# State-space layer on one Trainium2 core: its units sooner, one GELU over its output in place, GpSimd putting it in order

## The chip, the cores and the metric

The kernel runs on one core of a Trainium2 chip, in a single launch. The metric is device time in microseconds (us), lower is better. Three runs of the kernel before took 2256.18, 2250.8 and 2256.09 us (median 2256.09).

## The reference

One layer of a hybrid trunk over 2048 tokens of width 1024, in float32. A normalised input is projected; 512 of the projected columns go through a diagonal complex state-space scan (32 channel groups of 16), 1536 are queries, keys and values of chunked attention with 8 heads. Both outputs are normalised, joined and projected, and a SwiGLU feed-forward follows.

```python
states = associative_scan(combine, (lam_bar, b_bar @ u))     # per group: 64 complex states
y = Re(c_mat @ states) + d_skip * u
y = gelu(y)
y = y * sigmoid(y @ w_glu + b_glu)                           # GLU
x = x + concat(rmsnorm(y), rmsnorm(attention)) @ w_out
x = x + (silu(h2 @ w_gate) * (h2 @ w_up)) @ w_down
```

## The kernel before

Every product runs as three matmuls on values that are split into a high and a low part (fp32r), so TensorE (PE) carries most of the work. A split is a cast by ScalarE (ACT), which writes the high part, and a subtraction by VectorE (DVE), which writes the low part (`split`, L153). PE's instructions run in the order in which the program is written; those of the other engines are put in order when the kernel is built, and each engine then works through its own list strictly in turn.

The middle of the program is `att_phase`: 128 attention steps (4 blocks of 512 tokens, 4 pairs of heads, 2 heads, 4 query tiles), about 4 us each. For a step, PE computes scores (tile `sc`), DVE adds a bias and takes the minimum (`s`, `mn`, L874), ACT takes the exponential (L877); two steps later PE transposes the result (`pt`, L79, a single buffer), ACT casts it (`pth`, L892) and DVE forms the rest (`ptl`, L893). Every fourth step there are 16 matmuls with the values (`pj`), whose halves ACT and DVE add (`yt` L916, `ya` L917). Since `pt` has one buffer, PE's transposes of a step wait for the `ptl` of the step before.

Between these, in each step, `Unit.advance` runs pieces of other work on PE ("units"): the projections of later blocks (`pf`), and the state-space layer in 8 units of 4 groups each. A state-space unit has a front (`ssm_front`): SP loads its input `U` and a matrix `Bst`, PE runs 4 matmuls, ACT copies the result into `X` (8 copies, L584), GpSimd (POOL) scans `X` in place (L598 to L610) and sends the states to `XG` (L632, DMA); and a back (`ssm_back`): matmuls of `U` and `XG`, ACT copies the result over `U` (L652), and a DMA writes it to `y` in HBM (L654). `X`, `XG`, `U`, `Bst` have one buffer each; the input of units 2, 4 and 6 lies in `rsn`, a tile of another phase. The tables `SX` and `SY` (L661, L662) give the steps at which the fronts and backs start. SP issues all loads and most stores from one queue, in list order.

From step `OPEN` = 119 on, the first pieces of the next phase (`mix_phase`) run as units inside the last attention steps: the pool `aw` (projection weights and hidden tiles such as `hi0x`, `lo0x`) is released, 512 KB by 512 KB `y` is fetched into `yr` (4 DMAs, L1046), gate weights `sg` are loaded and split (`wgh`, `wgl`), and from step `GSTART` = 122 on a block of 512 tokens is taken with one GELU (L1058) that also turns the layout from (j, chunk) to (chunk, j):

```python
nc.scalar.activation(yt[:, s].rearrange("p f (c j) -> p f c j", j=L), yv[:, s].rearrange("p f j c -> p f c j"), AF.Gelu_apprx_tanh)
```

It reads one element in 128. The result `ys` is split into `gh` and `gl`, and `glu` (16 pieces, 3 matmuls each on `pf`) follows; `ya` loads bring the attention output, whose squares (`sq`, `sg`, L1031 to L1035) feed a norm. The GELU and the exponential need different tables on ACT, so each change brings an ACT_TABLE_LOAD. The next block's GELU comes four steps later. Behind the last step PE goes on with tile `big`.

Of the kernel before, what the change touches and what calls it, by code (L numbers as in the profile page):

```python
# [10 lines left out]
F32R = mybir.dt.float32r  # L11
# [5 lines left out]
P = 128  # L17
# [5 lines left out]
L = 8  # L23
NC = SEQ // L
# [8 lines left out]
LAG = 2  # L33
NSMALL = 100
WB = 3
OPEN, GSTART = 119, 122
R1 = 13
SGB = 2
RA1, RA2 = 2, 12
QS = 4, 5, 6, 7, 0, 1, 2, 3  # L40
HTA = -12, -9
HTS = -8, -6
# [51 lines left out]
def f32(ap):  # L94
    return ap.bitcast(F32)
# [462 lines left out]
        yield  # L558


def ssm_front(k, p, psum, S, b, eng):

    nc = k.nc

    def load(out, in_):
        ins = nc.sync.dma_start(out, in_)
        if b == 0:
            k.tc.keep_in_program_order(ins)

    U = S["rsn"][:, : GB * NC].rearrange("p (g c) -> p g c", g=GB) if b and b % 2 == 0 else k.t(p, "U", [P, GB, NC])[:]  # L570
    k.U[b] = U
    load(U.rearrange("p g t -> p (g t)"), S["u"].rearrange("j (c g) n t -> (j c) (g n t)", c=CH)[:, GB * NC * b : GB * NC * (b + 1)])
    bst = k.t(p, "Bst", [P, GB, P])
    load(bst[:].rearrange("p g m -> p (g m)"), S["bst"][b // 2][:, (b % 2) * GB * P : (b % 2 + 1) * GB * P])
    yield

    X = k.t(p, "X", [P, 2, GP, NC])
    for q in range(GP):
        ps = k.t(psum, "pj", [P, 2, NC], bufs=2)
        for g2 in range(2):  # L580
            k.ta.matmul(ps[:, g2, :], bst[:, 2 * q + g2, :], U[:, 2 * q + g2, :], start=True, stop=True)
        for g2 in range(2):
            for c in range(2):
                nc.scalar.copy(X[g2 * NS : (g2 + 1) * NS, c, q, :], ps[c * NS : (c + 1) * NS, g2, :])  # L584
        yield

    a8 = S["a8"]
    qs = slice(GP * b, GP * b + GP)
    Xk = X[:].rearrange("p r q (k s) -> p r q k s", s=8)
    Xe = Xk[:, :, :, :, 7].rearrange("p r q (a b) -> p r q a b", b=8)  # L590

    def step(dst, src, e, n):

        ar = a8[:, 0, qs, (0, 7, 15)[e]].unsqueeze(1).to_broadcast([P, 2, GP]).unsqueeze(3).to_broadcast([P, 2, GP, n])
        aw = S["sw"][:, e, :, qs].unsqueeze(3).to_broadcast([P, 2, GP, n])
        t = k.t(p, "st1", [P, 2, GP, NC // 8])
        t2 = k.t(p, "st2", [P, 2, GP, NC // 8])
        eng.tensor_tensor(t[:, :, :, :n], src, ar, op=ALU.mult)  # L598
        eng.tensor_tensor(t2[:, :, :, :n], src[:, ::-1], aw, op=ALU.mult)
        eng.tensor_tensor(dst, dst, t[:, :, :, :n], op=ALU.add)  # L600
        eng.tensor_tensor(dst, dst, t2[:, :, :, :n], op=ALU.add)

    def carry(dst, end, i0, n):

        for c in range(2):
            for e in range(2):
                t = k.t(p, "fx", [P, GP, NC // 8, 7])[:, :, :n]
                pw = a8[:, c if e == 0 else 1 - c, qs, i0 : i0 + 7].unsqueeze(2).to_broadcast([P, GP, n, 7])
                eng.tensor_tensor(t, end[:, e].unsqueeze(3).to_broadcast([P, GP, n, 7]), pw, op=ALU.mult)
                eng.tensor_tensor(dst[:, c], dst[:, c], t, op=ALU.subtract if e == 1 and c == 0 else ALU.add)  # L610
# [12 lines left out]
    yield from carry(Xk[:, :, :, 1:, :7], Xk[:, :, :, : NC // 8 - 1, 7], 0, NC // 8 - 1)  # L623

    if b == 0:
        k.XG = k.t(p, "XG", [P, GB, NC])
        nc.gpsimd.memset(k.XG[:, :, 0:1], 0.0)
    XG = k.XG
    XGv = XG[:].rearrange("p (q g) c -> p q g c", g=2)
    for g2 in range(2):  # L630
        for c in range(2):
            eng.dma_start(XGv[c * NS : (c + 1) * NS, :, g2, 1:], X[g2 * NS : (g2 + 1) * NS, c, :, : NC - 1])  # L632
    yield


def ssm_back(k, p, psum, S, b):

    nc = k.nc
    gs = slice(GB * b, GB * b + GB)
    tm = k.t(p, "Tm", [P, GB, P])  # L640
    nc.sync.dma_start(tm[:], S["tm"][:, gs])
    vm = k.t(p, "Vm", [P, GB, P])
    nc.sync.dma_start(vm[:], S["v"].rearrange("q g c n m -> (c n) (q g) m")[:, gs, CH:])
    yield
# [13 lines left out]
SSM_F = 1 + GP + 7 + 7 + 3 + 4 + 1  # L658
SSM_B = 1 + GP + 1
ST = 2, 10  # L660
SX = 4, 24, 35, 48, 61, 74, 87, 100  # L661
SY = 20, 36, 49, 62, 75, 88, 101, 114  # L662


class Unit:
# [21 lines left out]
def att_phase(k, ident, S, aw, x0, roots):  # L687

    tc, nc, io, pfs = k.tc, k.nc, k.io, k.pfs
    with ExitStack() as cx:  # L690
# [271 lines left out]
        k.U = {}  # L962
        units.append(Unit(shifted_taps(k, S), L, *ST))
        for b in range(NG // GB):
            units.append(Unit(ssm_front(k, sp, psum, S, b, k.ssm_eng), SSM_F, SX[b], SX[b] + 9, SX[b] - 2 if b == 0 else 2 if b == 1 else 5, light=SL))
            units.append(Unit(ssm_back(k, sp, psum, S, b), SSM_B, SY[b], SY[b] + 2, 6, light=SL))
        N = len(steps)
        for s in range(N + LAG + 2):
            if s == OPEN:
                aw.release()  # L970
                mix = mix_phase(k, S, lambda: k.t(pfs, "pf", [P, 512]))
                units += [Unit(islice(mix, MIX_N), MIX_N, GSTART, N + LAG, GSTART - OPEN)]
            if s == GSTART:
                sp.release()
# [12 lines left out]
        yield mix  # L987


PY, PZ = 8, 1  # L990
MIX_N = 17 + PY + PZ


def mix_phase(k, S, bank):
# [3 lines left out]
    with ExitStack() as cx:  # L998
# [49 lines left out]
        def load(sb, one=False):  # L1048
# [4 lines left out]
            if sb and sb % 2 == 0:  # L1053
                fetch(sb)
            yv = b.yr = yrs[0][:, :, :, (sb % 2) * 64 : (sb % 2 + 1) * 64]
            fs = [slice(0, 4)] if one else [slice(f, f + 1) for f in range(4)]
            for s in fs:
                nc.scalar.activation(yt[:, s].rearrange("p f (c j) -> p f c j", j=L), yv[:, s].rearrange("p f j c -> p f c j"), AF.Gelu_apprx_tanh)  # L1058
# [91 lines left out]
            yield  # L1150

        def next_block(sb):
            b = load(sb)
            load_a(b, sb)
            for _ in glu(b, big):
                pass
            return b
# [7 lines left out]
                for i in range(8):  # L1165
                    yield t[:, i * SB : (i + 1) * SB]

        fetch(0)
        load_wg()
        yield  # L1170
        mw = rx.enter_context(tc.tile_pool(name="mw", reuse_waits="tile", bufs=2, side="right"))
        wr = rx.enter_context(tc.tile_pool(name="wr", reuse_waits="tile", bufs=2, side="right"))
        b = load(0, True)
        load_a(b, 0)
        raws = [load_wo(n, wr, "xt") for n in range(2)]
        for _ in range(PY):
            yield
        for n, _ in enumerate(glu(b, bank, True)):
            if n == RA1:
                rstd1(b, 0, bank())  # L1180
            if n == RA2:
# [1 line left out]
                spread(k, te, pb, b.o[0], 0)  # L1183
                rstd2(b, 0, pb[:])
            yield
        nxt = load(1, True)
        for _ in range(PZ):
            yield

        def bk():  # L1190
            nonlocal psum
# [554 lines left out]
```

## Time and profile before

| | |
|---|---|
| profiled execution | 2247.43 us |
| its span | 2245.7 us (1.7 us lie around it) |
| median of 3 runs | 2256.09 us |
| PE, DVE, ACT, POOL busy | 2155.6, 1543.3, 1004.6, 352.4 us |
| mean granted TensorE clock | 0.988 |

The prediction quotes the rows. In a row of the timeline stand the start in us from the span's start, the duration, engine, line, operation, tiles (out<-in) and shape, and in brackets how long the engine had been idle before it and whom it waited for. In a row of windows stand the stretch, its length, the busy time of PE, PE's weight loads, DVE, ACT and POOL with their instruction counts, the granted TensorE clock (1.00 is full), the share of the DMA engines and GB/s.

### The profile page before, as it was taken

What the parts mean: (1) busy time and instruction counts of PE and PEld (TensorE: products, weight loads), DVE (VectorE), ACT (ScalarE), POOL (GpSimd) and SP (SyncE); (2) the same over time, 40 slices, a digit from 0 to 9 for tenths busy, and PEclk for the clock granted to TensorE, in tenths of its full rate; (3) what the DMA queues carried; (4) which work ended last, traced back from release to release, by engine and by line L of the source; (5) the groups of instructions that cost most, each with busy time, mean ns of one, the idle gap of its engine ahead of it and who ended that gap; (6) DMA issues with size and microseconds to landing.
All of it is one profiled execution on the core that took longest, in us unless ns stands there. A gap on an engine that the chain in (4) does not pass through costs nothing.

```text
span 2245.7 us, 30154 instructions
## 1 busy us (share of the span) xinstructions
PE 2155.6 (96%) x10632; PEld 1817.4 (81%) x10632; DVE 1543.3 (69%) x2706; ACT 1004.6 (45%) x1667; POOL 352.4 (16%) x827
## 2 busy tenths in 40 slices
PE   8998899999997999999999999999999999999997
PEld 6777788899986788788888887888888788888886
DVE  7756666555557766777766678767666477689776
ACT  5455555556557642443333335333333343353322
POOL 2246576656500000000000000000000100000000
PEclk9999999999998999999999999999999999999999
DMA  8878876666652435845655557646333395465652
GB/s 281 251 244 275 280 220 204 202 192 199 190 166 99 155 113 181 288 136 155 198 168 194 191 182 268 210 144 213 117 100 112 122 383 192 160 228 177 220 175 76
DMA packets 194744, 430.16 MB, mean 192 GB/s; under 512 B 19872, under 2 KB 38352, under 8 KB 187488
## 3 DMA queue, kind: packets, MB, share of 16 engines
q1 hardware_dynamic: 186944, 403.32, 54.4%
q0 software_dynamic: 7648, 24.92, 3.6%
q8 instruction: 83, 1.36, 0.2%
q14 instruction: 69, 0.57, 0.1%
HBM read 288.95 MB, written 131.10 MB: 187 GB/s over the span
## 4 chain that ended last, share of the span: by engine, by line
PE 81%; DVE 7%; DMA 4%; ACT 3%; issue 2%; SPq 0%; DVEq 0%; ACTq 0%
PE X L76 20%; PE ps L76 19%; PE Y L76 10%; PE pf L76 10%; PE big L76 7%; PE W L76 5%; PE pj L76 4%; PE pt L79 2%; PE sc L76 2%; DMA lo<-hc 1%; DMA xt<-in_xt 1%; DVE ptl L893 1%; DMA x<-xt 0%; DVE s L874 0%; DVE lo L153 0%
## 5 line engine op out<-in xcount | busy, mean ns | idle before, releaser
L76 PE MATMUL X<-hi,c 128*128 128x512 f32 x1408 | 449.8, 390 | 6.7 <-DVE c L153 3.9
L76 PE MATMUL ps<-hd,hd 128*128 128x512 f32 (+1 forms) x1968 | 428.1, 379 | 3.1 <-DVE hd L153 2.0
L76 PEld LDWEIGHTS ps<-hd,hd 128*128 128x128 f32 x1968 | 356.4, 188 | 73.3 <-DVE hd L153 2.7
L76 PEld LDWEIGHTS X<-hi,c 128*128 128x128 f32 x1408 | 264.5, 188 | 63.2 <-DVE c L153 4.7
L76 PE MATMUL X<-lo,c 128*128 128x512 f32 x704 | 274.4, 390 | 0.0
L153 ACT CAST hd<-hd 128x1536 fp32r<-128x1536 f32 (+1 forms) x106 | 147.5, 1394 | 229.9 <-DMA hd<-hq 175.5
L76 PE MATMUL Y<-hi,c 128*128 128x512 f32 x704 | 224.8, 390 | 3.1 <-DVE u L1421 2.5
L153 DVE TENSOR_TENSOR hd<-hd 128x1536 fp32r<-128x1536 f32 (+1 forms) x106 | 174.0, 1643 | 38.0 <-ACT hd L153 37.7
L153 DVE TENSOR_TENSOR c<-S,c 128x512 fp32r<-128x512 f32 x176 | 120.8, 687 | 100.1 <-ACT c L153 99.8
L1525 POOL DMA_DIRECT2D hd<-hq x7 | 5.3, 755 | 1161.5 <-PE X L76 1148.8
L1417 ACT COPY u<-X 128x512 f32<-128x512 f32 x132 | 77.3, 586 | 197.7 <-PE X L76 197.7
L153 ACT CAST c<-S 128x512 fp32r<-128x512 f32 x176 | 109.4, 621 | 120.5 <-PE Y L76 61.6
L76 PE MATMUL big<-m,woh 128*128 128x512 f32 x512 | 160.1, 394 | 0.0
L76 PEld LDWEIGHTS Y<-hi,c 128*128 128x128 f32 x704 | 132.4, 188 | 31.9 <-DVE u L1421 3.3
L1559 DVE TENSOR_TENSOR acc<-acc,ps 128x512 f32<-128x512 f32 x196 | 129.6, 680 | 37.3 <-PE ps L76 37.1
L76 PEld LDWEIGHTS X<-lo,c 128*128 128x128 f32 x704 | 132.4, 188 | 27.4
L76 PE MATMUL pf<-hi,w 128*128 128x512 f32 x416 | 149.3, 411 | 0.0
L153 ACT CAST c<-raw 128x512 fp32r<-128x512 f32 x132 | 82.2, 623 | 147.7 <-PE Y L76 70.6
L76 PE MATMUL Y<-lo,c 128*128 128x512 f32 x352 | 137.2, 390 | 0.0
L893 DVE TENSOR_TENSOR ptl<-pt,pth 128x640 fp32r<-128x640 f32 (+3 forms) x152 | 98.2, 646 | 55.2 <-ACT pth L892 53.8
L877 ACT ACTIVATE s<-s,mn 128x640 f32<-128x640 f32 (+4 forms) x128 | 98.0, 765 | 61.1 <-DVE mn L874 57.7
L892 ACT CAST pth<-pt 128x640 fp32r<-128x640 f32 (+3 forms) x152 | 83.6, 550 | 84.2 <-PE pt L79 79.5
(448 smaller groups left out, 4267.9 us busy)
## 6 DMA issues: line engine op xcount, KB each, us to landing
w<-wss SPq DMA_DIRECT2D x36, 1024.0 KB, 6.1
hq<-g SPq DMA_DIRECT2D x140, 256.0 KB, 2.1
hd<-hq SPq DMA_DIRECT2D x35, 768.0 KB, 4.4
hd<-wc SPq DMA_DIRECT2D x35, 768.0 KB, 5.9
raw<-in_w_gate SPq DMA_DIRECT2D x44, 512.0 KB, 3.7
raw<-in_w_up SPq DMA_DIRECT2D x44, 512.0 KB, 4.1
wc<-px SPq DMA_DIRECT2D x66, 256.0 KB, 3.4
wss<-w SPq DMA_DIRECT2D x12, 1024.0 KB, 6.0
```

Of the source, the lines that this page charges most:

```text
L76: return self.tc.keep_in_program_order(self.tc.nc.tensor.matmul(*a, **b))
L79: return self.tc.keep_in_program_order(self.tc.nc.tensor.transpose(*a, **b))
L153: return nc.scalar.copy(hi, raw), nc.vector.tensor_tensor(lo, raw, f32(hi), op=ALU.subtract)
L877: nc.scalar.activation(s[:, :nk], s[:, :nk], AF.Exp, bias=mn[:], scale=-1.0, accum_out=sums[sb, pr][:, hh, qp : qp + 1])
L892: nc.scalar.copy(pth[:, a:b, qp, :], pt[:, a:b, :])
L893: nc.vector.tensor_tensor(ptl[:, a:b, qp, :], pt[:, a:b, :], f32(pth[:, a:b, qp, :]), op=ALU.subtract)
L1417: nc.scalar.copy(u[:], ps[:])
L1525: (nc.gpsimd if aside else nc.sync).dma_start(f32(lo), src.rearrange("g p c -> p g c"))
L1559: V.tensor_tensor(a, a, ps[:], op=ALU.add)
```

## The change

1. The state-space units start sooner. Unit 1's input goes into two dead tiles of `aw` (`hi0x`, `lo0x`, 2 DMAs) and is read a second time into `U` at its back, so its front can run before unit 0's back; all later fronts and backs move ten steps up, with loads four steps ahead.
2. At step 107 the pool of the state-space units is released and `y` for the first 1024 tokens is fetched into a new tile `y0` (4 DMAs, L987); at step 111 one GELU runs over all of it in place, 128x4096 (L989), pinned in program order.
3. `take` (POOL copies of 128x512, L1079) replaces the two GELUs of the first two blocks; `glu` starts at step 121 with three pieces before the `y0` pool is given back and the `ya` loads come. The second block's split comes after the GLU.

```diff
-OPEN, GSTART = 119, 122
+FETCH, OPEN, GSTART = 107, 119, 121
-RA1, RA2 = 2, 12
+RA0, RA1, RA2 = 3, 10, 14
...
-    U = S["rsn"][:, : GB * NC].rearrange("p (g c) -> p g c", g=GB) if b and b % 2 == 0 else k.t(p, "U", [P, GB, NC])[:]
+    if b == 1:
+        us = [lent(q).rearrange("p (g c) -> p g c", g=2) for q in range(GP)]
+        for q in range(GP):
+            load(us[q], ssm_input(S, b, slice(q, q + 1)))
+    else:
...
 def ssm_back(k, p, psum, S, b):
+    if b == 1:
+        k.U[b] = k.t(p, "U", [P, GB, NC])[:]
+        nc.sync.dma_start(k.U[b], ssm_input(S, b))
...
-SX = 4, 24, 35, 48, 61, 74, 87, 100
-SY = 20, 36, 49, 62, 75, 88, 101, 114
+SX = 4, 19, 31, 42, 54, 66, 78, 91
+SY = 20, 32, 43, 55, 67, 79, 92, 104
...
+            if s == FETCH:
+                sp.release()
+                k.my0 = tc.alloc_tile_pool(name="my0", reuse_waits="tile", bufs=1)
+                k.y0 = k.t(k.my0, "y0", [P, 4, L, 128])
+                for f in range(4):
+                    nc.sync.dma_start(k.y0[:, f], S["y"][:, f * P : (f + 1) * P, :128].rearrange("j p t -> p j t"))
+            if s == FETCH + 4:
+                tc.keep_in_program_order(nc.scalar.activation(k.y0[:], k.y0[:], AF.Gelu_apprx_tanh))
...
-MIX_N = 17 + PY + PZ
+MIX_N = 19
...
+                if sb < 2:
+                    nc.gpsimd.tensor_copy(yo, yv[:, f].rearrange("p j c -> p c j"))
+                else:
+                    nc.scalar.activation(yo, b.yr[:, f].rearrange("p j c -> p c j"), AF.Gelu_apprx_tanh)
...
-        fetch(0)
         load_wg()
+        yrs[0] = k.t(my, "yr", [P, 4, L, 128])
+        b = load(take(0))
+        nxt = take(1)
         yield
+        yield
+        g = glu(b, bank, True)
+        for _ in range(RA0):
+            next(g)
+            yield
+        k.my0.release()
...
-        b = load(0, True)
         load_a(b, 0)
...
-        nxt = load(1, True)
+        load(nxt)
+        yield
```

On ACT, around step 111, before: the value half of step 107 is copied (`yt`), then transposes, exponentials and casts follow each other (numbers behind a tile's name count the tiles).

```order
L877 ACTIVATE s_7492,sm_7195<-s_7492,mn_7493 128x640
L916 COPY yt_7514<-pj_7497 64x512
L892 CAST pth_7517<-pt_7519 128x5x128
L834 CAST v_1628_7462<-pf_7466 128x4x64
L892 CAST pth_7517<-pt_7557 128x5x128
L877 ACTIVATE s_7553,sm_7195<-s_7553,mn_7554 128x640
L834 CAST v_1629_7463<-pf_7535 128x4x64
```

And there after the change (lines have moved on by 13):

```order
L890 ACTIVATE s_7518,sm_7279<-s_7518,mn_7519 128x640
L929 COPY yt_7540<-pj_7523 64x512
L905 CAST pth_7543<-pt_7545 128x5x128
L847 CAST v_1633_7488<-pf_7492 128x4x64
L989 ACT_TABLE_LOAD
L989 ACTIVATE y_1617_7402<-y_1617_7402 128x4096
L890 ACT_TABLE_LOAD
L890 ACTIVATE s_7580,sm_7279<-s_7580,mn_7581 128x640
L905 CAST pth_7543<-pt_7584 128x5x128
L847 CAST v_1634_7489<-pf_7561 128x4x64
```

Between the exponential of step 110 and that of step 111 now stand two table loads and the GELU, ahead also of the `pth` that came before that exponential.

On DVE, from step 119's minimum on, before:

```order
L874 ISA s_7906,mn_7907<-sc_7901,nbb_1554 128x640
L874 ISA mn_7907 128x1
L893 TENSOR_TENSOR ptl_7878<-pt_7910,pth_7877 128x5x128
L800 TENSOR_TENSOR k_1682_7758<-pf_7812,k_1682_7758 64x512
L874 ISA s_7964,mn_7965<-sc_7959,nba_107 128x640
```

And there after the change, up to the minimum of step 120:

```order
L887 ISA s_7920,mn_7921<-sc_7915,nbb_1554 128x640
L887 ISA mn_7921 128x1
L153 TENSOR_TENSOR gl_1727_7975<-ys_7969,gh_1726_7974 128x512
L813 TENSOR_TENSOR k_1685_7773<-pf_7826,k_1685_7773 64x512
L906 TENSOR_TENSOR ptl_7892<-pt_7924,pth_7891 128x5x128
L153 TENSOR_TENSOR gl_1729_7979<-ys_7969,gh_1728_7978 128x512
L153 TENSOR_TENSOR gl_1731_7983<-ys_7969,gh_1730_7982 128x512
L153 TENSOR_TENSOR wgl_1713_7945<-sg_7946,wgh_1712_7944 128x512
L153 TENSOR_TENSOR wgl_1716_7951<-sg_7952,wgh_1715_7950 128x512
L153 TENSOR_TENSOR gl_1733_7987<-ys_7969,gh_1732_7986 128x512
L887 ISA s_8000,mn_8001<-sc_7995,nba_107 128x640
```

Six splits, which before stood behind the minimum of step 123, are now ahead of that of step 120: four of the block (`gl`) and two of the gate weights (`wgl`).

On ACT, from step 121's exponential on, before:

```order
L877 ACTIVATE s_7982,sm_7966<-s_7982,mn_7983 128x640
L877 ACTIVATE s_8002,sm_7966<-s_8002,mn_8003 128x640
L1058 ACT_TABLE_LOAD
L1058 ACTIVATE ys_8046<-yr_7930 128x2048
L153 CAST wgh_1710_7935<-sg_7937 128x512
L153 CAST wgh_1713_7941<-sg_7943 128x512
L916 COPY yt_8027<-pj_8010 64x512
L892 CAST pth_8030<-pt_8032 128x5x128
```

And there after the change:

```order
L890 ACTIVATE s_8018,sm_8002<-s_8018,mn_8019 128x640
L918 COPY rb_8047<-rs_8045 128x512
L1052 ACTIVATE sg_8126<-ya_1761_8117 128x512
L1052 ACTIVATE sg_8129<-ya_1762_8118 128x512
L890 ACTIVATE s_8041,sm_8002<-s_8041,mn_8042 128x640
L1052 ACTIVATE sg_8132<-ya_1763_8119 128x512
L929 COPY yt_8066<-pj_8049 64x512
L905 CAST pth_8069<-pt_8071 128x5x128
```

The table load and the GELU between step 122's exponential and the `pth` behind it are gone, squares of the attention output stand around it, and the casts of gate weights have moved ahead.

More of the change, by code (lines that the diff above doesn't have):

```diff
@@ L558, in shifted_taps, with ssm_input, ssm_front @@
         yield
-def ssm_front(k, p, psum, S, b, eng):
+def ssm_input(S, b, q=slice(0, GP)):
+    return S["u"].rearrange("j (c g) n t -> (j c) g (n t)", c=CH)[:, GB * b : GB * b + GB][:, 2 * q.start : 2 * q.stop]
+def ssm_front(k, p, psum, S, b, eng, lent):
     nc = k.nc
@@ L568, in load @@
             k.tc.keep_in_program_order(ins)
-    U = S["rsn"][:, : GB * NC].rearrange("p (g c) -> p g c", g=GB) if b and b % 2 == 0 else k.t(p, "U", [P, GB, NC])[:]
-    k.U[b] = U
-    load(U.rearrange("p g t -> p (g t)"), S["u"].rearrange("j (c g) n t -> (j c) (g n t)", c=CH)[:, GB * NC * b : GB * NC * (b + 1)])
+    if b == 1:
[3 more added lines that the diff above has]
+    else:
+        U = S["rsn"][:, : GB * NC].rearrange("p (g c) -> p g c", g=GB) if b and b % 2 == 0 else k.t(p, "U", [P, GB, NC])[:]
+        k.U[b] = U
+        us = [U[:, 2 * q : 2 * q + 2] for q in range(GP)]
+        load(U, ssm_input(S, b))
     bst = k.t(p, "Bst", [P, GB, P])
@@ L580, in ssm_front @@
         for g2 in range(2):
-            k.ta.matmul(ps[:, g2, :], bst[:, 2 * q + g2, :], U[:, 2 * q + g2, :], start=True, stop=True)
+            k.ta.matmul(ps[:, g2, :], bst[:, 2 * q + g2, :], us[q][:, g2, :], start=True, stop=True)
         for g2 in range(2):
@@ L964, in att_phase @@
         for b in range(NG // GB):
-            units.append(Unit(ssm_front(k, sp, psum, S, b, k.ssm_eng), SSM_F, SX[b], SX[b] + 9, SX[b] - 2 if b == 0 else 2 if b == 1 else 5, light=SL))
+            units.append(Unit(ssm_front(k, sp, psum, S, b, k.ssm_eng, lambda q: f32(k.t(aw, ("hi0x", "lo0x")[q], [P, SB], F32R)[:])), SSM_F, SX[b], SX[b] + 9, SX[b] - 2 if b == 0 else 4, light=SL))
             units.append(Unit(ssm_back(k, sp, psum, S, b), SSM_B, SY[b], SY[b] + 2, 6, light=SL))
@@ L987, in att_phase @@
         yield mix
-PY, PZ = 8, 1
-MIX_N = 17 + PY + PZ
+MIX_N = 19
 def mix_phase(k, S, bank):
@@ L1046, in fetch, with take @@
                 nc.sync.dma_start(yrs[0][:, f], S["y"][:, f * P : (f + 1) * P, sb * 64 : sb * 64 + 128].rearrange("j p t -> p j t"))
-        def load(sb, one=False):
+        def take(sb):
             b = B()
@@ L1052, in load @@
             b.ys, b.g = [yt[:, f] for f in range(4)], []
-            if sb and sb % 2 == 0:
+            if sb < 2:
+                yv = k.y0[:, :, :, sb * 64 : sb * 64 + 64]
+            elif sb == 2:
                 fetch(sb)
[L1055 to L1058, printed above, removed]
+            b.yr = yrs[0][:, :, :, (sb % 2) * 64 : (sb % 2 + 1) * 64]
+            for f in range(4):
+                yo = b.ys[f].rearrange("p (c j) -> p c j", j=L)
+                if sb < 2:
+                    nc.gpsimd.tensor_copy(yo, yv[:, f].rearrange("p j c -> p c j"))
+                else:
+                    nc.scalar.activation(yo, b.yr[:, f].rearrange("p j c -> p c j"), AF.Gelu_apprx_tanh)
+            return b
+        def load(b):
             for f in range(4):
@@ L1152, in next_block @@
         def next_block(sb):
-            b = load(sb)
+            b = load(take(sb))
             load_a(b, sb)
@@ L1166, in pre_tiles @@
                     yield t[:, i * SB : (i + 1) * SB]
-        fetch(0)
         load_wg()
+        yrs[0] = k.t(my, "yr", [P, 4, L, 128])
+        b = load(take(0))
+        nxt = take(1)
         yield
+        yield
[4 more added lines that the diff above has]
+        k.my0.release()
         mw = rx.enter_context(tc.tile_pool(name="mw", reuse_waits="tile", bufs=2, side="right"))
         wr = rx.enter_context(tc.tile_pool(name="wr", reuse_waits="tile", bufs=2, side="right"))
-        b = load(0, True)
         load_a(b, 0)
         raws = [load_wo(n, wr, "xt") for n in range(2)]
-        for _ in range(PY):
-            yield
-        for n, _ in enumerate(glu(b, bank, True)):
+        for n, _ in enumerate(g, RA0):
             if n == RA1:
@@ L1185, in mix_phase @@
             yield
-        nxt = load(1, True)
-        for _ in range(PZ):
-            yield
+        load(nxt)
+        yield
         def bk():
```

2 lines of the change are left out of this document (removed).

## The prediction

> **What bounds the kernel now.** I read the page's first two parts, then the chain of work that ended last.
>
> ```profile
> PE 2155.6 (96%) x10632; PEld 1817.4 (81%) x10632; DVE 1543.3 (69%) x2706; ACT 1004.6 (45%) x1667; POOL 352.4 (16%) x827
> PE   8998899999997999999999999999999999999997
> PEclk9999999999998999999999999999999999999999
> PE 81%; DVE 7%; DMA 4%; ACT 3%; issue 2%; SPq 0%; DVEq 0%; ACTq 0%
> ```
>
> PE is busy for 2155.6 of 2245.7 us, so all its idle time is 90.1 us, and no edit that leaves PE's work alone can win more than that and what a throttled clock costs. The change adds no product, so everything hangs on where PE waits. The thirteenth slice (674 to 730 us) is one such place, and its clock is lower too: there the attention ends and the mixing phase begins. The windows show how special it is.
>
> ```profile
> 400.00:640.00 240.00, 238.88 (x1529) 219.29 (x1528) 131.16 (x237) 136.20 (x274) 139.40 (x352) 1.00 0.62 186
> 660.70:713.65 52.95, 36.74 (x199) 30.94 (x200) 35.42 (x73) 42.53 (x59) 0.00 (x0) 0.87 0.35 110
> 713.65:739.55 25.90, 23.32 (x105) 18.35 (x104) 25.34 (x47) 18.78 (x25) 0.00 (x0) 1.00 0.61 211
> 676.50:690.10 13.60, 6.93 (x24) 5.97 (x24) 8.43 (x14) 13.55 (x19) 0.00 (x0) 0.50 0.39 133
> ```
>
> From 400 to 640 us PE has 1.1 us idle in 240: state-space units that run there cost nothing, but nothing can be won there either. From 660.70 (the minimum of step 119) to 713.65 PE is idle for 16.2 us, and for 13.6 us of it the granted clock is one half, so that 6.93 us of PE work should have been 3.5. In the last attention steps PE waits for `ptl`, and these are the waits:
>
> ```profile
> 677.41 1.30 PE L79 MATMUL pt<-ident,s 128*128 128x128 f32 x5 [6.14 <-DVE ptl L893]
> 685.53 1.30 PE L79 MATMUL pt<-ident,s 128*128 128x128 f32 x5 [5.75 <-DVE ptl L893]
> 691.62 0.77 PE L79 MATMUL pt<-ident,s 128*128 128x128 f32 x5 [1.25 <-DVE ptl L893]
> ```
>
> DVE is only the last link. ACT's timeline shows what stands in front of the `pth` that `ptl` needs:
>
> ```profile
> 668.86 1.28 ACT L1058 ACT_TABLE_LOAD   x1
> 670.15 3.72 ACT L1058 ACTIVATE ys<-yr 128x2048 f32<-128x2048 f32 x1
> 680.39 1.28 ACT L877 ACT_TABLE_LOAD   x1
> 681.69 0.83 ACT L877 ACTIVATE s<-s,mn 128x640 f32<-128x640 f32 x1
> 685.05 1.28 ACT L1058 ACT_TABLE_LOAD   x1
> 686.35 3.79 ACT L1058 ACTIVATE ys<-yr 128x2048 f32<-128x2048 f32 x1
> 690.04 0.67 ACT L892 CAST pth<-pt 128x640 fp32r<-128x640 f32 x1
> ```
>
> Two GELUs of 3.7 us with their table loads, and the splits that depend on them, sit in ACT's list between exponentials and `pth` casts, and DVE idles just behind them:
>
> ```profile
> 670.88 0.82 DVE L874 CUSTOM_DVE_ANT_0 s<-sc,nba 128x640 f32<-128x640 f32 x1 [3.06 <-PE sc L76]
> 674.40 1.29 DVE L153 TENSOR_TENSOR wgl<-sg,wgh 128x512 fp32r<-128x512 f32 x2 [2.70 <-ACT wgh L153]
> 690.74 0.82 DVE L893 TENSOR_TENSOR ptl<-pt,pth 128x640 fp32r<-128x640 f32 x1 [5.36 <-ACT pth L892]
> ```
>
> **Term 1, the end of attention (steps 119 to 129): -12.5 us.** The GELUs with the two switches to their table and one of the two back take 1.28+3.72+1.28+1.28+3.79 = 11.35 us from ACT in this stretch (the last switch back, 1.28 as well, goes too). ACT falls from 42.53 to about 30 us of work. DVE keeps the same instructions in another order, 35.42 us, and becomes the longest; PE has 36.74 less 3.5, about 33.3 at full clock. In the next stretch, 713.65 to 739.55, DVE was busy for 25.34 of 25.90 us, 98%, with PE beside it: at that density DVE's 35.42 us would take 36.2, so at most 16.8 of the 52.95 us can go. Walking through the new lists by hand, with the durations of these rows, I find PE idle for 1.3 us before step 120's scores, 1.35 before its transposes, 3.35 before step 121's scores and about 0.4 later: DVE now has six splits of 0.62 to 0.65 us each ahead of the minimum of step 120, and the transposes and scores behind wait for it. That makes 6.4 us in place of 16.2 and 3.5 at half clock, 13.3 less; a wait of 3.35 can halve the clock again, so I take 12.5. Bounds: 16 at DVE's density, and 7 if DVE's splits stretch beside POOL (below). The new copies on POOL cost nothing by themselves, since POOL is idle in these windows; the new wait is that the `ya` loads stand in SP's queue until POOL's last copy, with the second half of `sg` behind them. The squares and the later `wgh` casts on ACT wait for these, and the `pth` casts behind them; 0.9 us of waits I put there (in the 6.4).
>
> **Term 2, the GELU at step 111: +6.6 us.** Here PE has no slack to hide it. Around it ACT and PE ran like this; the last row is the sigmoid that reads runs of 64 elements:
>
> ```profile
> 621.70 0.37 ACT L834 CAST v<-pf 128x256 fp32r<-128x256 f32 x1
> 624.27 0.69 ACT L892 CAST pth<-pt 128x640 fp32r<-128x640 f32 x1 [2.20 <-PE pt L79]
> 624.86 0.83 ACT L877 ACTIVATE s<-s,mn 128x640 f32<-128x640 f32 x1
> 626.10 0.71 PE L79 MATMUL pt<-ident,s 128*128 128x128 f32 x5
> L1087 ACT ACTIVATE yr<-yr x2: 1910/1914/1919, 711.7 to 731.3; 128x2048 f32<-128x2048 f32 x2
> ```
>
> ACT is free at 622.07. A load of 1.28, a GELU of 4096 elements in a row (twice 1.914, 3.83) and the load back (1.28) end at 628.46; the exponential of step 111 now comes first (0.74), then `pth` (0.69), then DVE's `ptl` (0.82): about 630.95, and PE's transposes of step 112, which ran at 626.10, start then. That is 4.85 us of idle PE. Behind each long wait the clock fell by half for a multiple of 3.4 us; one such stretch costs 1.7, so 6.6. The lower bound is 4.85 without it; the upper takes the GELU's price per element from the strided one (3.72 for 2048, 7.4 in all): 8.5 us idle, 10.2 with the clock. I stay with the contiguous row, since this GELU runs through memory in order. What the Trainium skill says speaks against the term: "ScalarE: Activation LUTs", section "What ACT_TABLE_LOAD costs", has for each switch of table the load and about 1.38 us of draining behind it. By that the two switches here would cost 2.8 us more and the whole sum would be 2.8 nearer to zero. This trace does not agree: the GELU at 670.15 and the exponential at 681.69 begin 0.01 to 0.02 us after their loads end.
>
> The GELU also needs its data. Unit 7's `y` is written about 602.5, where SP issued a weight load before, and these are the landing times:
>
> ```profile
> 602.09 0.33 SPq L716 DMA_DIRECT2D w<-wss  x1
> y<-U SPq DMA_DIRECT2D x5, 512.0 KB, 4.9
> yr<-y SPq DMA_DIRECT2D x8, 512.0 KB, 6.3
> ```
>
> The write lands near 607.5, the last two fetches leave about 613 behind loads of keys, and land near 619.5, four us before the GELU could start at 623.35: hidden, with that margin.
>
> **Term 3, the early part: -3.0 us.** Unit 1's front moves from step 24 to 19, past queries' stores and `xt` loads on SP. What goes:
>
> ```profile
> 239.59 0.77 PE L76 MATMUL pj<-U,Bst 128*128 128x256 f32 x1 [2.61 <-DMA Bst<-bsts]
> 239.60:243.00 3.40, 3.40 (x9) 2.77 (x9) 2.34 (x4) 1.77 (x5) 0.00 (x0) 0.50 1.06 325
> L584 ACT COPY X<-pj x64: 363/367/371, 159.3 to 583.0; 64x256 f32<-64x256 f32 x64
> 283.83 1.26 PE L79 MATMUL pt<-ident,s 128*128 128x128 f32 x5 [3.11 <-DVE ptl L893]
> ```
>
> The wait of 2.61 for `Bst` and the half clock behind it (1.7) disappear, 4.3 us, since the loads are now asked for four steps ahead. On the other side eight copies of 0.367 us (2.9 in all) come onto ACT in steps 19 and 20, beside unit 0's back; I charge 1.3 of them to PE (bounds 0 and 2.9). The wait of 3.11 at 283.83 I leave: hidden tiles and a state-space unit meet there as before. In its place may come another of that size, so the bounds of the term are -4.3 and +0.5. The other fronts and backs move within stretches where PE was never idle.
>
> **Sum.** -12.5 + 6.6 - 3.0 = -8.9 us: the profiled execution would go from 2247.43 to 2238.5. It lies 8.7 us below the median of the runs, and I carry over the difference: 2256.1 - 8.9 = 2247.2.
>
> **Rivals.** (A) *The GELU at step 111 is dearer.* It costs its strided price, or waits for its fetch, and PE stands for 8.5 to 10 us there. For it: a `y` that comes 4 us late eats the margin. Against it: the contiguous row. The sum becomes -5.3 to -4, about 2251.5.
>
> (B) *POOL's copies stretch DVE and the end of attention is bound by it.* Beside POOL's scan, DVE's operations on two tiles in SBUF took far longer than alone:
>
> ```profile
> 279.30 2.13 DVE L749 SCALAR_TENSOR_TENSOR raw<-raw,g_mix,rsn 128x512 f32<-128x512 f32 x1
> L749 DVE SCALAR_TENSOR_TENSOR raw<-raw,g_mix,rsn x12: 740/745/2132, 237.4 to 392.7; 128x512 f32<-128x512 f32 x12
> ```
>
> If the four `gl` splits, of two SBUF tiles each, meet the eight copies, each takes 1.4 us more, all on DVE's path ahead of step 120's minimum: 5.6 us, and the sum is -3.3, about 2252.8. Against it: POOL's copies can mostly be done before DVE comes to the splits. The Trainium skill states such a rule ("SBUF — State Buffer", section "Who interferes with whom"): a DVE instruction with two SBUF inputs and a GpSimd instruction that reads SBUF shut each other out for a whole instruction. By that rule the time would be this rival's; the 2.13 us row agrees with it.
>
> (C) *Slower: the scans can't follow the fronts.* `X` has one buffer, so a front's eight copies on ACT wait until POOL has scanned and sent the unit before. Unit 1 before took this long on POOL, and steps 19 and 31, where units 1 and 2 now start, were these:
>
> ```profile
> 244.85 0.50 POOL L598 TENSOR_TENSOR st<-X,a 128x128 f32<-128x128 f32 x1 [38.84 <-ACT X L584]
> 284.23 1.23 POOL L632 DMA_DIRECT2D XG<-X  x2 [0.30 <-POOL X L610]
> 214.24 0.72 ACT L877 ACTIVATE s<-s,mn 128x512 f32<-128x512 f32 x1 [0.84 <-DVE mn L874]
> 264.98 0.73 ACT L877 ACTIVATE s<-s,mn 128x512 f32<-128x512 f32 x1 [0.51 <-DVE mn L874]
> XG<-X POOLq DMA_DIRECT2D x32, 127.5 KB, 4.7
> ```
>
> From scan to last send 40.6 us, 4.7 to land, about 3 for the matmuls and copies: 48.3, against 50.7 us between the two steps. The margin is 2.4 us. If a unit takes over 51 us, ACT stands at the copies, exponentials and `pth` stand behind, and PE loses the lateness and 1.7 at half clock; four of the six hand-overs are as tight. At 3 us late each it costs 4 x 4.7 = 19 us, and the sum is +10, about 2266. Against it: from 400 to 640 us POOL was busy for 139.40 of 240 us, so that on average there is slack.
>
> **How the numbers follow.** Forecast (sum between -13 and -5) 0.47; A 0.14; B 0.12; C 0.22; and 0.05 that the end of attention reaches DVE's density and the GELU its lower bound, -15 or so. About 0.3%, 6.8 us, is what a measurement of this kernel tells from no change. Of the forecast's 0.47, 0.40 lie beyond it; with the 0.05 that is 0.45 faster. The rest of the forecast, A and B make 0.33 the same; C gives 0.22 slower. The range takes in the bounds of the three terms (-16 - 4.3 + 4.85 = -15.5 to -7 + 10.2 + 0.5 = +3.7), with runs that spread by 5.4 us, and most of C: 2236 to 2264.
>
> **What would show it.** Right: no table load between 655 and 700 us, step 119 to `big` in about 41 us in place of 54, the clock at 1.00 there; PE idle once for about 5 us before step 112's transposes; no wait for `Bst` near 240. Wrong: ACT idle at `X` copies behind POOL or DMA at steps 31 to 66 (C), a GELU of over 5 us or idle ACT before it (A), `gl` splits above 1 us (B).

## The result: 0.2% slower, and the profile after

The changed kernel takes 2256.97 us (median of 18 runs, 2251.33 to 2260.72) against 2252.44 of the kernel before (18 runs): ratio 1.0019, 95% interval 1.001 to 1.0028, that is 4 us slower where 8.9 us less had been forecast. The profiled execution took 2254.93 us, span 2253.1. Below stand the engines' row of the page after, the windows of three stretches before and after, and the last steps of attention after. There the minimum of step 119 starts at 671.95 (660.70 before), and tile `big` at 717.47 (713.39 before), so that 671.95 to 717.73 is the stretch that was 660.70 to 713.65. First after:

```profile
PE 2163.2 (96%) x10632; PEld 1824.7 (81%) x10632; DVE 1543.5 (69%) x2706; ACT 997.3 (44%) x1664; POOL 370.6 (16%) x835
255.00:300.00 45.00, 37.34 (x226) 33.42 (x225) 24.50 (x47) 20.85 (x51) 31.45 (x60) 0.96 0.80 267
300.00:420.00 120.00, 114.30 (x698) 102.78 (x696) 75.68 (x130) 68.65 (x136) 87.30 (x212) 0.99 0.70 215
500.00:560.00 60.00, 56.76 (x339) 50.95 (x339) 36.02 (x61) 34.63 (x70) 37.18 (x93) 1.00 0.65 196
671.95:717.73 45.78, 36.74 (x199) 31.67 (x200) 37.36 (x76) 29.52 (x53) 0.00 (x0) 0.89 0.27 93
```

Then before:

```profile
255.00:300.00 45.00, 41.67 (x254) 37.27 (x254) 31.16 (x56) 24.17 (x56) 33.90 (x83) 0.96 0.84 262
300.00:420.00 120.00, 113.95 (x701) 102.93 (x700) 75.31 (x127) 68.20 (x137) 77.11 (x186) 0.99 0.66 204
500.00:560.00 60.00, 59.87 (x370) 54.03 (x369) 36.75 (x67) 36.45 (x73) 39.95 (x94) 1.00 0.70 202
```

The end did get shorter: 45.78 us in place of 52.95, with PE's 36.74 us unchanged and ACT down from 42.53 to 29.52. The loss stands ahead of it, in part where PE had hardly been idle: 255 to 300 us has 7.7 us of idle PE in place of 3.3, and 500 to 560 us 3.2 in place of 0.1. From 300 to 420 us both have about 6.

The start of a step's exponential on ACT, after minus before, shows where the two drift apart. The steps are chosen so that the same units are done in both.

| step | after - before, us | what lies in between |
|---|---|---|
| 19 | +0.1 | |
| 30 | -2.3 | unit 1's front, early |
| 54 | +5.4 | units 2 and 3 |
| 66 | +2.4 | before had a wait of 4.1 at 379.76 |
| 104 | +5.2 | units 5 to 7 |
| 118 | +11.3 | the GELU at step 111 |
| 127 | +1.8 | most of the end |
| `big` on PE | +4.1 | the rest of it |

So the schedule costs 5.2 us up to step 104, the GELU 6.1, and the end gives 7.2 back: 4.1 in all, close to what the runs show. One trace is a rough measure of the early part, though. `unit2_later` and `gelu_tanh` below give PE and ACT the same lists up to step 107, and at step 104 their traces stand 6.4 us apart. Behind `big` the trace after is another 3.4 us late; that is no sign of the change, since `ssm_alone` below, with the program of before there, is 4.9 us late. PE's longest waits of the trace after, from 255 us to the last steps, in its timeline:

```profile
275.17 0.70 PE L76 MATMUL pj<-U,Tm 128*128 128x256 f32 x2 [3.15 <-ACT X L594]
284.73 0.41 PE L76 MATMUL sc<-k,q2h 128*128 128x320 f32 x1 [1.96 <-DVE mn L887]
311.76 0.76 PE L79 MATMUL pt<-ident,s 128*128 128x128 f32 x5 [2.32 <-DVE ptl L906]
402.35 0.77 PE L79 MATMUL pt<-ident,s 128*128 128x128 f32 x5 [2.64 <-DVE ptl L906]
531.49 0.41 PE L76 MATMUL sc<-k,q2h 128*128 128x320 f32 x1 [3.24 <-DVE k L813]
639.41 1.30 PE L79 MATMUL pt<-ident,s 128*128 128x128 f32 x5 [4.57 <-DVE ptl L906]
678.77 0.64 PE L76 MATMUL sc<-k,q2h 128*128 128x320 f32 x1 [2.98 <-DVE mn L887]
713.16 0.50 PE L76 MATMUL pj<-ptl,v 128*128 128x512 f32 x1 [2.21 <-DVE ptl L906]
```

The first one starts a series, and ACT and POOL show its cause (ACT's rows, then POOL's):

```profile
266.54 0.37 ACT L847 CAST v<-pf 128x256 fp32r<-128x256 f32 x1 [0.39 <-PE pf L76]
273.61 3.03 ACT L594 COPY X<-pj 64x256 f32<-64x256 f32 x8 [6.70 <-DMA XG<-X]
276.83 0.83 ACT L890 ACTIVATE s<-s,mn 128x640 f32<-128x640 f32 x1
```

```profile
264.48 1.23 POOL L642 DMA_DIRECT2D XG<-X  x2 [0.30 <-POOL X L620]
276.73 0.46 POOL L608 TENSOR_TENSOR st<-X,a 128x128 f32<-128x128 f32 x1 [11.02 <-ACT X L594]
```

POOL has sent unit 1's last states at 265.71. Unit 2's eight copies stand at the head of ACT's list from 266.91 on, but `X` is free only when that sending has landed, at 273.6, nearly 8 us after its issue. Step 32's exponential, whose list place is behind the copies, starts at 276.83, 8.1 us later than before. This is rival C, at the one hand-over of steps 19 and 31.

### The profile page after: what moved, and what is told of

It reads as the page before. It is cut to its first block, busy times and chain, and to the rows that moved or that the text cites. A ratio compares the mean times of both kernels' runs of the same rounds, so it can differ in the third digit from the quotient of the medians.

```text
span 2253.1 us, 30164 instructions
## 1 busy us (share of the span) xinstructions
PE 2163.2 (96%) x10632; PEld 1824.7 (81%) x10632; DVE 1543.5 (69%) x2706; ACT 997.3 (44%) x1664; POOL 370.6 (16%) x835
## 4 chain that ended last, share of the span: by engine, by line
PE 80%; DVE 5%; DMA 4%; POOL 4%; issue 2%; ACT 2%; SPq 0%; DVEq 0%; ACTq 0%; POOLq 0%
PE X L76 21%; PE ps L76 17%; PE Y L76 10%; PE pf L76 9%; PE big L76 9%; PE W L76 5%; PE pj L76 4%; PE pt L79 2%; PE sc L76 2%; DMA acc<-x 2%; POOL X L611 1%; POOL X L610 1%; POOL st L608 1%; POOL st L609 1%; POOL fx L619 0%
```

## The experiments

Two theories. **S**: the new schedule itself costs, above all because unit 2's front at step 31 comes before unit 1's states are sent (S1); because DVE's hidden-tile work now falls beside POOL's scan (S2), or, a theory that came up on the way, because loads crowd there (S3). **N**: the schedule is worth its -3 us, and the loss comes from the fetch and the GELU at its end. The ratios are to the kernel before; a hundredth of a per cent is 0.23 us.

**The schedule alone** (`ssm_alone`): the kernel before with this part of the diff, unit 1's lent tiles, its second read and the loads four steps ahead included. As the tables show, the fronts behind unit 0 move up by four to nine steps and the backs by four to ten, not by ten throughout.

```diff
-SX = 4, 24, 35, 48, 61, 74, 87, 100
-SY = 20, 36, 49, 62, 75, 88, 101, 114
+SX = 4, 19, 31, 42, 54, 66, 78, 91
+SY = 20, 32, 43, 55, 67, 79, 92, 104
```

> The kernel before with the new schedule of the state-space units only (SX, SY, unit 1's input in lent tiles, loads four steps ahead); the fetch, the GELUs and the end of attention stay as before. Theory S (the schedule itself costs): the trace after the change is 5.2 us behind the one before at step 104, so about +5 us, ratio 1.0022, with ACT idle for 6 us or more ahead of unit 2's copies into X near 270 us. Rival N (the schedule is worth its -3 us and the loss comes from the new fetch and GELU at its end): ratio 0.9987, and no such idle time.

Measured: 1.0034 (1.0021 to 1.0047), 7.7 us slower. Step 104 is 7.7 us late, and ACT waits ahead of unit 2's copies:

```profile
274.56 3.03 ACT L594 COPY X<-pj 64x256 f32<-64x256 f32 x8 [6.36 <-DMA XG<-X]
```

N is out: the schedule costs, without fetch and GELU.

**The end alone** (`end_alone`): the changed kernel with the units' schedule of before, so that the fetch and the GELU come later.

```diff
-FETCH, OPEN, GSTART = 107, 119, 121
+FETCH, OPEN, GSTART = 116, 119, 121
...
-            if s == FETCH + 4:
+            if s == FETCH + 3:
```

> The changed kernel with the schedule of the state-space units of before (SX, SY, one input), and so with the fetch at step 116 and the GELU at step 119 in place of 107 and 111. Theory S: nothing is lost up to step 114; GELU +6, end of attention -9: about -3 us, ratio 0.9987. Rival N: the end alone loses what the change loses, ratio 1.002 or more. A third case: at step 119 the GELU falls on the splits of the end, and the gain there shrinks to less than the GELU costs: ratio 1.000 to 1.001.

Measured: 0.9996 (0.9985 to 1.0007), no difference to the kernel before. The time alone doesn't rule out S's 0.9987, which lies in the interval; the trace speaks for the third case: from step 118 to `big` it loses 3.4 us where the changed kernel wins 7.2. At step 119 the GELU has the casts of `wgh` and `gh` behind it on ACT, all of them ahead of a `pth`, and PE's transposes wait for one long stretch (ACT's rows, then PE's):

```profile
663.11 3.62 ACT L976 ACTIVATE y<-y 128x4096 f32<-128x4096 f32 x1
669.90 2.17 ACT L153 CAST gh<-ys 128x512 fp32r<-128x512 f32 x4
673.80 0.69 ACT L892 CAST pth<-pt 128x640 fp32r<-128x640 f32 x1
```

```profile
679.23 1.30 PE L79 MATMUL pt<-ident,s 128*128 128x128 f32 x5 [14.46 <-DVE ptl L893]
```

Moving the GELU out of the end needs `y` early, and so the units early: the two parts belong together.

**Without the GELU** (`no_gelu`):

```diff
-            if s == FETCH + 4:
-                tc.keep_in_program_order(nc.scalar.activation(k.y0[:], k.y0[:], AF.Gelu_apprx_tanh))
```

> The changed kernel without the GELU at step 111 (the first two blocks go on without a GELU). If the GELU costs what the trace shows at its place (4.6 us of idle PE and half a clock window of 1.5), the time is 6 us below the changed kernel: about -1.6 us against before, ratio 0.9993. Rival: what is won at step 111 is lost again in steps 119 to 129, where DVE is the bound: ratio stays at 1.001 to 1.002.

Measured: 0.9985 (0.9975 to 0.9995). Against the changed kernel's 1.0019 that is 0.34% or 7.7 us less, and by the traces none of it is lost again up to `big`. Against `ssm_alone`, which has the same schedule and the old end, it is 0.49% or 11 us less (intervals together: 7 to 15): that is what the new end is worth without its GELU. The traces show 7.4 us of it from step 118 to `big`.

**Unit 2 and the units behind it two steps later** (`unit2_later`; the last front one step, its back not at all):

```diff
-SX = 4, 19, 31, 42, 54, 66, 78, 91
-SY = 20, 32, 43, 55, 67, 79, 92, 104
+SX = 4, 19, 33, 44, 56, 68, 80, 92
+SY = 20, 34, 45, 57, 69, 81, 93, 104
```

> The changed kernel with the fronts from unit 2 on two steps (unit 7: one step) later, SX = 4, 19, 33, 44, 56, 68, 80, 92 and SY = 20, 34, 45, 57, 69, 81, 93, 104. Theory S1 (unit 2's copies at step 31 wait for the sending of unit 1's states, 6.7 us of idle ACT and about 5 us of PE): the wait goes and the ratio falls to about 1.000. Rival S2 (the loss is DVE's, whose hidden-tile operations stretch beside POOL's scan, wherever they meet): other waits take its place, ratio 1.001 to 1.003.

Measured: 0.9968 (0.9955 to 0.998), 7 us faster than before, 11.5 below the changed kernel, more than S1 had put on the one wait. The copies now wait for nothing but PE, the waits at 311.76 and 402.35 have gone too, and step 104 is at -6.5 us. The later wait for `k` has not: PE waits 3.11 us near 518, in this faster kernel as well.

```profile
272.59 3.03 ACT L594 COPY X<-pj 64x256 f32<-64x256 f32 x8 [0.54 <-PE pj L76]
```

**One step later** (`unit2_one`), the same units: SX = 4, 19, 32, 43, 55, 67, 79, 92 and SY = 20, 33, 44, 56, 68, 80, 93, 104:

> The changed kernel with the fronts from unit 2 on one step later in place of two (SX = 4, 19, 32, 43, 55, 67, 79, 92; SY = 20, 33, 44, 56, 68, 80, 93, 104). By S1 the copies' wait of 6.7 us shrinks by a step of some 4 us: about half of what two steps won (ratio 0.9968), so 0.999 to 1.000. By S2 the place of POOL's last operations against the hidden tiles decides, and one step can be as good as two or no better than none.

Measured: 0.9983 (0.9973 to 0.9993), 8 us below the changed kernel. The copies still wait, a little less:

```profile
272.37 3.02 ACT L594 COPY X<-pj 64x256 f32<-64x256 f32 x8 [5.67 <-DMA XG<-X]
```

The wait shrank by 1 us only, yet most of the gain is there. Traces of the changed kernel's own schedule have 6.70, 6.36 and 4.86 (`no_gelu`), so that 5.67 is not even told from them. PE waits 2.0 us for the copies, in place of 3.15, and no longer for weights, and step 104 is at -3.0. S1 had 0.999 to 1.000, which the interval only touches; why one step brings more than half stays open.

**Without unit 1's sending** (`no_send1`), with nothing else moved:

```diff
-            eng.dma_start(XGv[c * NS : (c + 1) * NS, :, g2, 1:], X[g2 * NS : (g2 + 1) * NS, c, :, : NC - 1])
+            if b != 1:
+              eng.dma_start(XGv[c * NS : (c + 1) * NS, :, g2, 1:], X[g2 * NS : (g2 + 1) * NS, c, :, : NC - 1])
```

> The changed kernel without the sending of unit 1's states (its four DMAs into XG are left out, so that unit 1's back works on unit 0's states). Nothing else moves. Theory S1 (unit 2's copies at step 31 wait for that sending to land, 8 us after POOL issued it): ACT's 6.7 us of idle time at the copies goes, and with it about 5 us: ratio about 0.9997. If the later waits (2.3 us at step 39, 2.6 at step 59) are sequels of the late unit 2, up to 5 more, 0.9975. Rival S2 (DVE beside POOL's scan): the wait for X at step 31 is followed by the others all the same, ratio 1.001 or more.

Measured: 0.9975 (0.9965 to 0.9985), 10 us below the changed kernel. The copies start 6.4 us earlier and wait for PE alone:

```profile
267.24 3.02 ACT L594 COPY X<-pj 64x256 f32<-64x256 f32 x8 [0.55 <-PE pj L76]
```

With no unit moved, this says that unit 1's sending and those who wait for it are the cause of most of it, and not the new places of the later units. The one trace shows less: its span is 6 us shorter, 4 of them between steps 19 and 54.

**Without the carry** (`no_carry`): POOL's last 16 operations of each scan, from unit 1 on, are left out.

```diff
+                if b:
+                    continue
                 t = k.t(p, "fx", [P, GP, NC // 8, 7])[:, :, :n]
```

> The changed kernel without the carry of units 1 to 7, the last 16 of POOL's operations in each scan (their sums across chunks are left out); all sends stay, and POOL is done some 11 us sooner in each unit. S1's wait at step 31 goes here too, since unit 1's sending lands before unit 2's copies; what also goes is the stretch in which POOL's longest operations run beside DVE's hidden tiles (S2). If S2 is worth something of its own, the time lies below that without unit 1's sending (0.9975), and the waits for ptl and k near 402 and 531 us are gone: 0.995 to 0.997. If the late hand-over is all, 0.9975 or the hand-over's share that the trace shows (0.9995), with the wait for k near 531 us still there.

Measured: 1.0008 (0.9993 to 1.0024), a miss for every theory. The sending is done sooner and the copies wait for PE alone, but the sending now falls on weight loads, which from 240 to 262 us land 11.6 us after their issue (median; 7.1 in the changed kernel). PE waits for one of them, as its timeline shows:

```profile
262.03 0.80 PE L76 MATMUL pf<-w,hi0x 128*128 128x256 f32 x2 [5.17 <-DMA w<-wss]
```

So the DMA engines are a third party at this place. In the changed kernel SP issues the loads of unit 1's back and unit 2's front ahead of two weight loads; in `unit2_later` the weights come first. Two more runs part the front from the back.

**Unit 1's back alone later** (`back1_later`: SY = 20, 34, 43, ...) and **unit 2's front alone later** (`back1_early`: as `unit2_later`, but SY = 20, 32, 45, ...):

> The changed kernel with unit 1's back, and so its loads of 1 MB (Tm, U, Vm), two steps later (SY 32 to 34); all fronts stay. In the list of SP the weight loads w now stand ahead of them. Theory S3 (at steps 27 to 33 the loads of unit 1's back and unit 2's front stand ahead of the weights on SP, so that weights and unit 1's sending come late together): the waits for w near 260 us go, the sending lands sooner, and half of the loss or more goes: ratio 0.998 to 1.000. S1 (unit 2's front two steps too early, whatever else is loaded): the copies still wait 6 us and the ratio stays near 1.002.

> The kernel with unit 2 two steps later (0.9968), but with unit 1's back left at step 32, so that its loads stay ahead of the weights on SP while unit 2's front goes to 33. S1: the front alone makes the difference, 0.997. S3: the crowd of loads stays in part, 0.998 to 1.001, with a wait for w near 260 us.

Measured: 1.0028 (1.0015 to 1.0041) and 0.9996 (0.9985 to 1.0008). With the back later no wait for weights is left and the sending lands 1 us sooner, but the copies wait all the same, and PE, which would have had the back's matmuls to do meanwhile, waits longer (ACT's row, then PE's):

```profile
272.49 3.01 ACT L594 COPY X<-pj 64x256 f32<-64x256 f32 x8 [8.07 <-DMA XG<-X]
```

```profile
277.47 1.09 PE L79 MATMUL pt<-ident,s 128*128 128x128 f32 x4 [7.35 <-DVE ptl L906]
```

This is no faster than the changed kernel, so S3's 0.998 to 1.000 is out. With the front later, S1's 0.997 is missed, and no wait for `w` is seen; PE waits for the same sending itself, in the back's second matmul:

```profile
273.61 0.67 PE L76 MATMUL pj<-XG,Vm 128*128 128x256 f32 x2 [2.19 <-DMA XG<-X]
```

The landing near 273 us thus has two waiters, unit 2's copies at step 31 and unit 1's back at step 32, and of these schedules only those that shift both by two steps are free of it. S3, the crowd of loads, is not the loss by itself, and moving loads makes little of it: the last two sends took 8.2 us in the changed kernel, 7.5 with the back later and still 6.8 in `unit2_later`.

**The shifted schedule alone** (`ssm_alone_later`): `ssm_alone` with the SX and SY of `unit2_later`.

> The kernel before with the new schedule of the state-space units only, as in ssm_alone (ratio 1.0034), but with the fronts from unit 2 on two steps later, as in unit2_later. If the three parts add up (schedule +7.6 us, GELU about +8, end about -11 from the runs so far) and two steps take 11.5 from the first, the schedule alone is worth -4 us: ratio 0.998. Rival: the gain of unit2_later comes from how the later units meet the fetch and the end, and the schedule alone stays above 1.000.

Measured: 0.9989 (0.998 to 0.9999), -2.5 us. The same schedule, two steps wider at one place, turns from +7.7 to -2.5. That this is near term 3's -3.0 is no support for it, since the schedule is another.

**The GELU at step 115** (`gelu_115`): `unit2_later` with the GELU four steps later (`FETCH + 8`).

> The kernel with unit 2 two steps later (ratio 0.9968), and the GELU at step 115 in place of 111. At step 111 it costs 4.6 us of idle PE, since a step there has 3 us of PE work; steps 114 and 115 take 5.2 us each. If ACT's 6.2 us are hidden by the PE work of a step, about 2 us less are lost: ratio 0.996. Rival: the stall is set by the chain of exponential, cast and ptl and is the same anywhere: 0.9968. If POOL's copies now come too late for the splits of step 119: 0.998.

Measured: 0.9964 (0.995 to 0.9977), not told from 0.9968. PE's longest wait for `ptl` there falls from 4.57 to 3.6 us; whether that reaches the time stays open.

**The GELU with a tanh** (`gelu_tanh`): `unit2_later`, with this in place of the GELU, for eight pieces of 128x512 in as many steps, and 0.5 as factor in POOL's copies.

```diff
-            if s == FETCH + 4:
-                tc.keep_in_program_order(nc.scalar.activation(k.y0[:], k.y0[:], AF.Gelu_apprx_tanh))
...
+                tc.keep_in_program_order(nc.scalar.activation(t[:], t[:], AF.Tanh))
+                nc.vector.scalar_tensor_tensor(yf, t[:], 1.0, yf, op0=ALU.add, op1=ALU.mult)
...
+                nc.gpsimd.tensor_tensor(t[:], yf, yf, op=ALU.mult)
+                nc.gpsimd.tensor_scalar(t[:], t[:], 0.0356774081, 0.7978845608, op0=ALU.mult, op1=ALU.add)
+                nc.gpsimd.tensor_tensor(t[:], t[:], yf, op=ALU.mult)
```

> The kernel with unit 2 two steps later, and the GELU written out: POOL forms 0.798 y + 0.0357 y^3 in pieces of 512, ACT takes a hyperbolic tangent of each (eight of about 0.6 us in steps 110 to 117, with no change of table), DVE forms (t + 1) y, and POOL's copies halve it. If the step-111 stall is the price of the two table loads and the block of 4096 in one piece, it goes: 6 us, ratio about 0.994. If eight DVE operations beside POOL's stretch (1.4 us each) or POOL is late (some 3.5 us per piece and eight copies before step 119): 0.996 to 0.999.

Measured: 0.9942 (0.9929 to 0.9954), 13 us faster than before, 2238.54 us: the best of all, and 5.9 us below `unit2_later`. Between steps 104 and 118 the trace loses nothing (-0.2 at both), where `unit2_later` loses 6.2. From 611 to 652 us, steps 107 to 117, PE is never idle, and no table load stands among the tanhs:

```profile
L994 ACT ACTIVATE yg<-yg x8: 624/634/643, 620.6 to 650.8; 128x512 f32<-128x512 f32 x8
L995 DVE SCALAR_TENSOR_TENSOR y<-yg,y x8: 673/690/720, 621.3 to 651.7; 128x512 f32<-128x512 f32 x8
611.00:652.00 41.00, 41.00 (x285) 38.55 (x284) 29.86 (x55) 25.91 (x51) 30.29 (x27) 1.00 0.63 171
```

## Why the prediction was wrong, step by step

**Term 3 failed, in its sign.** It put -3.0 us on the schedule, "the other fronts and backs move within stretches where PE was never idle"; the schedule alone costs +7.7. The early front did what was said: at step 30 the trace is 2.3 us ahead, and the wait for `Bst` is gone. But a stretch in which PE was never idle was taken for a place where units are free, wherever they start. What keeps them free is the distance between the fronts, and rival C had that sum: 48.3 us for a unit against 50.7 between the steps. Each of its terms came out too small. In the event unit 1's copies were done and POOL began only at 220.28, 6.0 us into step 19 in place of about 3. From there to the last send it took 45.4 us in place of 40.6, and unit 2's copies could start 7.9 us behind that in place of 4.7. That is 59.3 us against 50.1 between the two steps: the margin of 2.4 became a shortfall of about 9.

```profile
220.28 0.46 POOL L608 TENSOR_TENSOR st<-X,a 128x128 f32<-128x128 f32 x1 [14.05 <-ACT X L594]
220.28:265.71 45.43, 40.02 (x211) 33.06 (x210) 31.49 (x73) 25.89 (x68) 41.72 (x88) 0.96 0.90 296
L610 POOL TENSOR_TENSOR X<-X,st 128x16 f32<-128x16 f32 x7 | 3.4, 491 | 0.0
XG<-X POOLq DMA_DIRECT2D x4, 127.5 KB, 7.5
```

And unit 1's scan before:

```profile
244.85:285.46 40.61, 36.34 (x232) 32.19 (x232) 28.57 (x59) 20.69 (x53) 36.90 (x88) 0.98 0.78 249
L600 POOL TENSOR_TENSOR X<-X,st 128x16 f32<-128x16 f32 x7 | 1.6, 230 | 0.0
```

POOL's part of this is a lengthening of its own operations: the same 88 took 41.72 us in place of 36.90, and the small additions (128x16) 491 ns each in the mean in place of 230. Scanning from step 19, POOL has more of DVE's work on hidden tiles beside it (13 operations, L762 and L764, in place of 8). That S2's meeting in this way also makes S1's hand-over later is likely, but no run takes that work away to show it.

C was weighed at 0.22 and priced for four hand-overs, each 3 us late, at 4.7 us each. One was late, the first, by 9 us; later copies waited for no sending. With its two waiters and what follows on them it cost some 10 us (7.7 against -2.5 for the schedule alone). Of the later waits the one for `k` near 531 us (3.2 us) fell to 1.8 without the carry, but stays at 3.1 in `unit2_later`; whatever S2 costs there, it is not what the two steps won.

**Term 2 was right.** +6.6 forecast; 6.1 us between steps 104 and 118, 7.7 by the runs. The GELU went at the contiguous price (3.63 us), PE waited 4.57 us where 4.85 had been worked out, and behind it the clock stood at 0.57 for 3.4 us, which is 1.5 us more:

```profile
630.67 1.28 ACT L989 ACT_TABLE_LOAD   x1
631.97 3.63 ACT L989 ACTIVATE y<-y 128x4096 f32<-128x4096 f32 x1
635.61 1.28 ACT L890 ACT_TABLE_LOAD   x1
636.91 0.83 ACT L890 ACTIVATE s<-s,mn 128x640 f32<-128x640 f32 x1
639.40:642.80 3.40, 3.39 (x18) 3.40 (x19) 1.02 (x2) 1.30 (x4) 0.33 (x1) 0.57 0.00 0
```

ACT was not idle just ahead of it, so the fetch had landed. Rival A didn't come, nor the 1.38 us of draining that the prediction quotes: the GELU starts 0.02 us after its load ends.

**Term 1 was right in kind and too large.** -12.5 forecast; -7.2 in the trace (45.78 in place of 52.95), -11 by the runs, with 7 to 15 as the interval. The waits of 1.3, 1.35 and 3.35 us came as 1.11, 1.33 and 2.98. Two things had been missed. Later waits stand with 0.4 us in the forecast's 6.4 (the 0.9 that its text puts on the `ya` loads doesn't fit into that) and came to 3.6: above all 1.04 at step 128's transposes and 2.21 before a value product, both where `ptl` stands behind scalings and splits on DVE. PE is idle for 9.04 us in all. And the 3.5 us at half clock were not won: PE's 199 matmuls took 36.74 us as before, at a granted clock of 0.89 in place of 0.87. From step 119's minimum to `big` it is 45.5 us, where about 41 had been named; before it was 52.7, not 54. Rival B didn't come: the splits `gl` took 0.69 us each, since POOL had copied the first block at 635.66 to 639.74, long before, and the second from 664.91 to 669.18, before DVE's first split at 672.70.

The terms of the trace, 5.2 + 6.1 - 7.2 = 4.1, agree with the 4 us of the runs. Those by the runs, 7.7 - 11 + 7.7 = 4.4, add up by construction, since each is the difference of two neighbours on the way from the kernel before to the changed one. That 2256.97 lies inside the range of 2236 to 2264 is luck in part: the base of three runs, 2256.09, was 3.7 us above the median of 18.

## What to carry to other kernels

That an engine was never idle in a stretch says what work there costs now; it doesn't say that the work may start elsewhere. For a chain with one buffer, take the whole time from one start to the buffer's release, the landing of its last DMA included, at the crowded place where it is to run, and compare it with the distance of the starts. A block of another function on the engine of the softmax cost 6 us here; in eight pieces and in a form that needs no other table it cost nothing that the trace shows. Which of the two did it was not tried.

## What the runs showed of the hardware

Unit 1's last two sends of 127.5 KB each landed after 4.1 us in the kernel before and after 8.2 in the changed one. The DMA engines were busy for 0.63 of that stretch before and for all of it after (first before, then after):

```profile
284.20:288.80 4.60, 4.60 (x17) 3.79 (x16) 3.56 (x7) 1.51 (x3) 1.23 (x2) 0.66 0.63 174
XG<-X POOLq DMA_DIRECT2D x2, 127.5 KB, 4.1
264.50:273.50 9.00, 7.51 (x56) 7.10 (x54) 1.81 (x6) 1.91 (x5) 1.20 (x2) 1.00 1.00 277
XG<-X POOLq DMA_DIRECT2D x2, 127.5 KB, 8.2
```

Weight loads of 1 MB beside sends that came earlier (`no_carry`) took 11.6 us in the median, in place of 7.1. Tanh and the exponential run from one table: eight tanhs among the exponentials, with no ACT_TABLE_LOAD. The Trainium skill has this in "ScalarE: Activation LUTs", section "Table sets: the hidden batching unit", and the trace agrees. In `gelu_tanh` DVE's eight operations on two SBUF tiles ran at 0.69 us, 0.72 at most. Four of them met one of POOL's operations, and in three of these POOL's was the one that got longer: the operations of 0.62 us to 1.17 and 0.94, and one of 1.30 to 1.63:

```profile
L1001 POOL TENSOR_SCALAR yg<-yg x8: 612/621/1167, 617.3 to 644.0; 128x512 f32<-128x512 f32 x8
L1002 POOL TENSOR_TENSOR yg<-yg,y x8: 1287/1301/1632, 618.7 to 644.8; 128x512 f32<-128x512 f32 x8
```

Beside the scan before it was DVE that got longer, to 2.13 us. What decides between the two was not tried.
